# A two-layer decoder on one core: each layer's last residual as 7 products of sums, with the weights' sums made by DMA steps due by a rate for each stage

## The chip, the cores and the metric

The kernel runs on one core of one Trainium2 chip. The metric is the device time of one execution in microseconds (us), as the median of several runs. Five engines work side by side on the core: TensorE (PE: matrix products; PEld is its load of the stationary operand), VectorE (DVE), ScalarE (ACT), GpSimd (POOL) and SyncE (SP), which here only issues DMA transfers.

## The reference, cut to what matters

```python
for layer in range(2):
    h = rmsnorm(x, norm_mix[layer])                 # x: 512 tokens x 1024
    z = h @ w_in[layer]                             # then a convolution, two attentions, gates
    x = x + (g_conv * y_conv + g_attn * y_nsa + g_mla * y_mla) @ w_out[layer]
    x = x + memory_cross_attention(rmsnorm(x, norm_xattn[layer]), ...)
    gate, up = jnp.split(rmsnorm(x, norm_ffn[layer]) @ w_gate_up[layer], 2, axis=-1)
    x = x + (jax.nn.silu(gate) * up) @ w_down[layer]    # 512 x 2816 times 2816 x 1024
return rmsnorm(x, norm_final)
```

All data is float32. The line that the change rewrites is the product with `w_down`, once per layer; FFN below is the 2816.

## The kernel before, in words

Every float32 product is made as three matmuls of halves: each operand is split into a high part (a cast on ACT, `hilo`, L92) and a low part (the difference, on DVE, L93), and high times high, high times low and low times high are accumulated in one bank of PSUM (L85 to L87, or L1143 to L1145 in `residual`). Weights come through three steps. `load` (L101) brings up to 1 MB into `raw`, of which there are two buffers, by a DMA that SP issues. `unit` splits 128x1024 of it into `wh` and `wl`, three buffers each. Then PE uses them.

A layer goes through these stages: the mix (`mix`: projection, convolution, both attentions, merges), the residual with `w_out`, the cross attention and its residual, the feed forward (gate and up), and the last residual with `w_down`. Instructions on an engine run in program order, which a scheduler has fixed by priorities.

Gate and up are already computed with 7 products in place of 8 (a 2x2 scheme on sums of quarters of both operands). The sums of quarters of `w_gate_up` are made in DRAM by `summed`: 128 DMA steps per layer, each a copy or an accumulating copy of 320 KB, in groups of 8 in which the fifth and sixth add to what the first two left, the seventh adds the fifth's result and the eighth the seventh's. POOL issues them (L356). `tick` is called after each third matmul and yields one step at each fifth call in layer 0 and at each sixth for layer 1, whose steps begin in layer 0's last residual. Each step also waits on the matmul it was tied to. POOL has other work in its queue as well: fills of `Pc` (L879) and `PTh` for the attentions, the power in each norm (L200, tile `rs`) and the stores of `x` to DRAM (`xd`, L1298).

In the last residual, `residual` walks over 22 k-tiles of 128. Each k-tile's unit of 128x1024 weights feeds 4 token tiles and 2 column halves, so 8 accumulators x 3 = 24 matmuls of 128x512, 528 per layer. `act` holds the activations, already split, in buffers that `keep_act` fills during the feed forward; at the end 8 additions (L1157) put the banks on `xs`, and `after` stores them or makes the final norm.

Of the kernel before, what the change touches and what calls it, by code (L numbers as in the profile page):

```python
# [9 lines left out]
F32 = mybir.dt.float32  # L10
# [8 lines left out]
T = 512  # L19
# [32 lines left out]
def kernel(ctx, tc, x, mem, positions, rel_bias, norm_mix, norm_xattn, norm_mem, norm_ffn, norm_final,  # L52
# [276 lines left out]
    def summed(l):  # L329

        W = w_gate_up[l]
        n, rows = FFN - 256, 64
        sums = [dr.tile([512, n], F32, name=f"sums{l}_{i}") for i in range(4)]

        def steps():
            for r, c in pairs(range(0, 512, rows), (0, n // 2)):
                s = [t[r:r + rows, c:c + n // 2] for t in sums]
                w = [[W[q + r:q + r + rows, o + 256 + c:o + 256 + c + n // 2] for q in (0, 512)] for o in (0, FFN)]  # L340
                for dst, src in ((s[0], w[1][0]), (s[2], w[0][0]), (s[1], w[0][0]), (s[3], w[0][1])):
                    yield dst, src, None
                for dst, src in ((s[0], w[1][1]), (s[2], w[1][0]), (s[1], s[0]), (s[3], s[1])):
                    yield dst, src, OP.add

        return sums, steps()
# [3 lines left out]
    paced = {"count": 0, "every": 1, "steps": iter(())}  # L350

    def tick(product):
        paced["count"] += 1
        if paced["count"] % paced["every"] == 0:
            for dst, src, op in islice(paced["steps"], 1):
                d = nc.gpsimd.dma_start(dst, src, accum_op=op) if op else nc.gpsimd.dma_start(dst, src)  # L356
# [4 lines left out]
    def mix(l, x_src, g_mix, x_now, more_x):  # L361
# [10 lines left out]

        tm_raw = [tm_load(0)]
# [719 lines left out]

        for _ in start(1):
            pump(3)
# [17 lines left out]

        run(merge_steps(1, w_branch_nsa[l], split4([o_nsa[0][:, k, :] for k in range(4)])))
# [54 lines left out]

    xin = x[0]  # L1170
# [3 lines left out]
    sums, paced["steps"] = summed(0)  # L1174
    paced["every"] = 5
    for l in range(L):
# [126 lines left out]
        assert not list(paced["steps"])  # L1303
        g_next = load_gain(norm_final if last else norm_mix[l + 1])
        act = []
        homes = ["op"] * 10 + ["ca"] * 2 + ["PT"] * 2 + ["gm", "h", "h", "u"] + ["o8"] * 2 + ["BT"] * 2
        size = {"o8": 4, "BT": 2}
        shared = {}

        def act_slots(m):  # L1310
            home = homes[m]
            if home == "PT":
                return new("PTh", dt=F32R, name="ah"), new("PTl", dt=F32R, name="al")
            if home == "h":

                k = 2 * (m - homes.index("h"))
                return hTh[:, k:k + 2, 256:512], hTl[:, k:k + 2, 256:512]
            if home == "u":
                return [new("u", (128, T + TAPS - 1), F32R, name="au")[:, 0:T] for _ in range(2)]
            if home in ("o8", "BT"):  # L1320
                i = shared.setdefault(home, [None, 0])
                r = []
                for _ in range(2):
                    if i[0] is None:
                        i[0], i[1] = new(home, (128, size[home], 512), F32R, name="a4"), 0
                    r.append(i[0][:, i[1], :])
                    i[1] += 1
                    if i[1] == size[home]:
                        i[0] = None
                return r  # L1330
            return new(home, dt=F32R, name="ah"), new(home, dt=F32R, name="al")

        def keep_act(m, a):
            ah, al = act_slots(m)
            hilo(ah, al, a.rearrange("p (a b) -> p a b", a=2) if len(ah.shape) == 3 else a)
            act.append((ah, al))
# [101 lines left out]
        if not last:  # L1438
            sums, paced["steps"] = summed(1)
            paced["every"] = 6  # L1440
# [64 lines left out]
```

## Time and profile before

| | before |
|---|---|
| median of 3 runs | 1943.12 us (1942.74 to 1944.12) |
| the profiled execution | 1943.2 us, of which the span that the profile covers is 1941.5 us |
| PE busy | 1913.9 us, 99% of the span |
| DVE, ACT, POOL busy | 1371.0, 979.2, 227.6 us |
| DMA queue of SP (weights) and queue of POOL (steps, stores) | 34.8% and 21.0% of 16 engines' span |
| first to last matmul start of layer 0's last residual | 855.09 to 975.65 us |

The profiled execution lies 0.1 us above the median, so its times can be used without correction. A busy time counts each instruction's own duration; PE's matmuls overlap, and what one costs is the distance between two starts.

### The profile page before, as it was taken

The numbers are of one execution on the slowest core, as the hardware profiler recorded it, in microseconds if no ns is written. First come the engines' busy times: TensorE is split into PE (matmuls) and PEld (weight loads), VectorE is DVE, ScalarE is ACT, GpSimd is POOL, SyncE is SP. The second block draws the span as 40 slices with busy tenths as digits, with TensorE's granted clock in tenths as the row PEclk, the third lists the DMA queues.
The fourth block names the chain that finished last, engine by engine and source line by source line (L and its number), as shares of the span: only waits on it lengthen the run. The fifth ranks groups of instructions, "written<-read, shape, count | busy, mean of one in ns | idle before, by whom it ended". The sixth has DMA issues, their size and how long they took to land.

```text
span 1941.5 us, 29100 instructions
## 1 busy us (share of the span) xinstructions
PE 1913.9 (99%) x11136; PEld 1674.5 (86%) x11136; DVE 1371.0 (71%) x2525; ACT 979.2 (50%) x1858; POOL 227.6 (12%) x380
## 2 busy tenths in 40 slices
PE   9999999999999999999999999999999999999998
PEld 8877888888887999998888878888888889999886
DVE  6989899764466877762279989986655677777523
ACT  5366557663355545541244755675634465545312
POOL 1211112112121000001211111111112010000000
PEclk9999999999999999999999999999999999999999
DMA  6676655567783455566666565445676525555531
GB/s 186 152 188 182 154 134 137 132 169 211 221 229 113 154 175 192 177 226 176 175 168 162 161 189 127 122 102 141 170 204 181 177 99 173 179 182 174 183 108 65
DMA packets 218871, 317.95 MB, mean 164 GB/s; under 512 B 14528, under 2 KB 172483, under 8 KB 218732
## 3 DMA queue, kind: packets, MB, share of 16 engines
q1 hardware_dynamic: 194028, 220.83, 34.8%
q0 software_dynamic: 21760, 88.10, 21.0%
q10 hardware_dynamic: 2944, 7.17, 1.1%
q8 instruction: 87, 1.43, 0.3%
q14 instruction: 52, 0.43, 0.1%
HBM read 307.64 MB, written 92.30 MB: 206 GB/s over the span
## 4 chain that ended last, share of the span: by engine, by line
PE 80%; DVE 8%; issue 5%; DMA 4%; ACT 3%; POOL 1%; SPq 0%; DVEq 0%; POOLq 0%; ACTq 0%
PE ps_mm L85 12%; PE ps_mm L87 12%; PE ps_mm L86 12%; PE ps_mm L1143 2%; PE ps_mm L1144 2%; PE ps_mm L1145 2%; PE ps_t L85 2%; PE ps_t L86 2%; PE ps_t L87 2%; PE ps_s L85 2%; PE ps_s L86 2%; PE ps_s L87 2%; DMA raw<-in_w_in_dram 2%; PE ps_t L960 2%; PE ps_t L1144 2%
## 5 line engine op out<-in xcount | busy, mean ns | idle before, releaser
L93 DVE TENSOR_TENSOR wl<-raw,wh 128x1024 fp32r<-128x1024 f32 (+5 forms) x382 | 451.2, 1185 | 377.2 <-ACT wh L92 375.7
L92 ACT CAST wh<-raw 128x1024 fp32r<-128x1024 f32 (+5 forms) x382 | 388.0, 1020 | 587.5 <-PE ps_pv L1145 198.7
L85 PE MATMUL ps_mm<-hTh,wh 128*128 128x512 f32 (+1 forms) x1152 | 415.4, 361 | 1.1 <-DVE kc L93 1.1
L87 PE MATMUL ps_mm<-hTh,wl 128*128 128x512 f32 (+1 forms) x1152 | 411.4, 358 | 0.8 <-DVE wl L93 0.8
L86 PE MATMUL ps_mm<-hTl,wh 128*128 128x512 f32 (+1 forms) x1152 | 412.0, 358 | 0.0
L87 PEld LDWEIGHTS ps_mm<-hTh,wl 128*128 128x128 f32 x1152 | 218.2, 190 | 33.4 <-DVE wl L93 1.9
L85 PEld LDWEIGHTS ps_mm<-hTh,wh 128*128 128x128 f32 x1152 | 218.5, 190 | 30.4 <-DVE kc L93 1.5
L86 PEld LDWEIGHTS ps_mm<-hTl,wh 128*128 128x128 f32 x1152 | 218.5, 190 | 26.5 <-issue 0.7
L356 POOL DMA_DIRECT2D sums<-in_w_gate_up_dram x192 | 119.6, 627 | 842.1 <-PE ps_mm L87 429.6
L463 DVE SCALAR_TENSOR_TENSOR ca<-u,vT,ca 128x512 f32<-128x512 f32 x240 | 177.1, 745 | 2.9
L923 ACT ACTIVATE P<-P,ss 128x512 f32<-128x512 f32 (+3 forms) x128 | 71.4, 558 | 55.9 <-DVE ss L920 55.0
L92 ACT CAST PTh<-ps_t 128x512 fp32r<-128x512 f32 (+4 forms) x136 | 70.4, 517 | 55.8 <-PE ps_t L960 45.0
L85 PE MATMUL ps_s<-rh,wh 128*128 128x256 f32 x320 | 90.6, 283 | 0.0
L86 PE MATMUL ps_s<-rl,wh 128*128 128x256 f32 x320 | 90.6, 283 | 0.0
L87 PE MATMUL ps_s<-rh,wl 128*128 128x256 f32 x320 | 90.6, 283 | 0.0
L356 POOL DMA_DIRECT2D sums<-sums x64 | 50.0, 782 | 275.4 <-PE ps_mm L87 130.1
L93 DVE TENSOR_TENSOR PTl<-ps_t,PTh 128x512 fp32r<-128x512 f32 (+2 forms) x120 | 71.3, 596 | 8.4 <-ACT PTh L92 7.5
L931 ACT ACTIVATE P<-P,sr 128x512 f32<-128x512 f32 (+3 forms) x128 | 63.1, 553 | 18.2 <-DVE sr L929 18.1
L85 PE MATMUL ps_mm<-op,wh 128*128 128x512 f32 (+1 forms) x192 | 68.7, 358 | 0.0
L86 PE MATMUL ps_mm<-op,wh 128*128 128x512 f32 (+1 forms) x192 | 68.2, 355 | 0.0
L87 PE MATMUL ps_mm<-op,wl 128*128 128x512 f32 (+1 forms) x192 | 68.1, 355 | 0.0
L200 POOL TENSOR_TENSOR rs<-rs,mhalf 128x1 f32<-128x1 f32 x32 | 23.1, 721 | 383.5 <-DVE rs L197 383.3
(553 smaller groups left out, 4574.1 us busy)
## 6 DMA issues: line engine op xcount, KB each, us to landing
sums<-in_w_gate_up_dram POOLq DMA_DIRECT2D x192, 320.0 KB, 4.4
raw<-sums SPq DMA_DIRECT2D x80, 512.0 KB
raw<-in_w_in_dram SPq DMA_DIRECT2D x32, 1024.0 KB
raw<-in_w_gate_up_dram SPq DMA_DIRECT2D x24, 1024.0 KB
raw<-in_w_down_dram SPq DMA_DIRECT2D x22, 1024.0 KB
sums<-sums POOLq DMA_DIRECT2D x64, 320.0 KB, 4.9
raw<-in_w_in_dram SPq DMA_DIRECT2D x26, 512.0 KB
raw<-in_w_gate_up_dram SPq DMA_DIRECT2D x20, 512.0 KB
```

Of the source, the lines that this page charges most:

```text
L85: nc.tensor.matmul(o, lh, rh, start=start, stop=False)
L86: nc.tensor.matmul(o, lh, rl, start=False, stop=False)
L87: tick(nc.tensor.matmul(o, ll, rh, start=False, stop=stop))
L92: nc.scalar.copy(hi, src)
L93: nc.vector.tensor_tensor(lo, src, f(hi), op=OP.subtract)
L356: d = nc.gpsimd.dma_start(dst, src, accum_op=op) if op else nc.gpsimd.dma_start(dst, src)
L463: nc.vector.scalar_tensor_tensor(c, u[:, j:j + T], cw[:, m, j:j + 1], c, op0=OP.mult, op1=OP.add)
L923: nc.scalar.activation(p[:, c], p[:, c], AF.Exp, bias=s[:, k:k + 1], scale=-1.0, accum_out=s[:, 4 + k:5 + k])
L931: nc.scalar.activation(P[k], P[k], AF.Copy, scale=r[:, k:k + 1])
L960: nc.tensor.transpose(tp[:, w:w + 128], P[k][:, j * 128:(j + 1) * 128], ident)
L1143: nc.tensor.matmul(o, xh, wh[:, r], start=k == 0, stop=False)
L1144: nc.tensor.matmul(o, xh, wl[:, r], start=False, stop=False)
```

## The change

The last residual becomes `down_residual`. The output is cut into token halves (256 tokens) and column halves (512), and the 2816 long sum into 11 pairs of k-tiles. Seven parts run in turn, each with its own pair of operands: sums of quarters of the activations on one side, quarters or sums of quarters of `w_down` on the other. A part has 11 pairs x 2 token tiles x 3 = 66 matmuls of 128x512, so a layer has 462. Each part loads its weights anew, in loads of 1 MB, 1 MB and 0.75 MB, and splits them in 5.5 units. Its results go to `xs` by additions after each part (`done`), some through a held tile `U`.

The sums of `w_down`'s quarters are 88 further DMA steps per layer (256 KB each), behind the 128 of gate and up. `tick` now adds a rate per call and issues a step when 1.0 is reached: 0.25 at the start of the mix, 0.35 in the attentions, 0.25 from the last merge to the cross attention, 0.05 in the feed forward, 0.06 in layer 0's last residual, where layer 1's steps begin.

`keep_act` multiplies into unsplit quarters, splits only two of the four sums that it keeps, and adds the sums by four 128x512 DVE additions per 4 m (256 hidden columns each pair of m) at low priority. The other five sums of activations are split in `down_residual`, a part ahead (`fourth`, `split`).

```diff
+        W, V = w_gate_up[l], w_down[l]
         n, rows = FFN - 256, 64
-        sums = [dr.tile([512, n], F32, name=f"sums{l}_{i}") for i in range(4)]
+        up = [dr.tile([512, n], F32, name=f"up{l}_{i}") for i in range(4)]
+        down = [dr.tile([128, FFN // 256, 512], F32, name=f"down{l}_{i}") for i in range(4 if l in seven else 0)]
+        def added(s, w):
+            for dst, src in ((s[0], w[1][0]), (s[2], w[0][0]), (s[1], w[0][0]), (s[3], w[0][1])):
+                yield dst, src, None
+            for dst, src in ((s[0], w[1][1]), (s[2], w[1][0]), (s[1], s[0]), (s[3], s[1])):
+                yield dst, src, OP.add
...
+            for j in range(FFN // 256 if down else 0):
+                yield from added([t[:, j, :] for t in down],
+                                 [[V[(2 * j + e) * 128:(2 * j + e + 1) * 128, o:o + 512] for e in range(2)]
+                                  for o in (0, 512)])
...
-        paced["count"] += 1
-        if paced["count"] % paced["every"] == 0:
+        paced["due"] += paced["rate"]
+        if paced["due"] >= 1.0:
+            paced["due"] -= 1.0
...
+        paced["rate"] = 0.25
...
+        paced["rate"] = 0.35
...
+        paced["rate"] = 0.25
...
+    def down_residual(W, sums, kept, xs, more_x, after):
+        N = len(kept)
+        low = slice(0, 512), slice(512, 1024)
+        quarters = W.rearrange("(j e p) c -> e p j c", e=2, p=128)
+        b11, b12, b21, b22 = ([k[e][i] for k in kept] for e in range(2) for i in range(2))
+        e11, e21 = ([(k[e][2], k[e][3]) for k in kept] for e in range(2))
+        def split(v):
+            h, lo = (new("op", (128, 2, 256), F32R, name=n)[:, 0:v.shape[1], :] for n in ("th", "tl"))
+            hilo(h, lo, v)
+            return h, lo
+        def fourth(n):
+            v = new("P", (128, 2, 256), name="t2")[:, 0:b11[n].shape[1], :]
+            nc.vector.scalar_tensor_tensor(v, b11[n], -1.0, b22[n], op0=OP.mult, op1=OP.subtract)
+            return split(v)
...
+        parts = [(quarters[0][:, :, low[0]], lambda n: None), (quarters[1][:, :, low[0]], fourth), (sums[1], lambda n: split(b12[n])),
+                 (sums[2], lambda n: split(b21[n])), (quarters[1][:, :, low[1]], lambda n: split(b11[n])),
+                 (sums[0], lambda n: split(b22[n])), (sums[3], lambda n: None)]
+        tags = (("t", "t"), ("s", "s"), ("mm", "mm"), ("mm", "pv"), ("t", "t"), ("s", "s"), ("mm", "mm"))
+        U = [None] * 2
...
+        def done(i, t, p):
+            x, y = xs[t], xs[2 + t]
+            if i == 0:
+                U[t] = new("op", name="U")
+                nc.scalar.copy(U[t], p)
+                add(x[0], x[0], p)
+            elif i == 1:
+                add(x[0], x[0], p)
+            elif i == 2:
+                add(U[t], U[t], p)
+                later(y[0], U[t])
+            elif i == 3:
+                add(U[t], U[t], p)
+                later(x[1], U[t], OP.subtract)
+                later(y[1], U[t], OP.subtract)
+            elif i == 4:
+                add(x[1], x[1], p, OP.subtract)
+                after(t)
+            elif i == 5:
+                add(y[0], y[0], p)
+                add(y[1], y[1], p, OP.subtract)
+            else:
+                add(y[0], y[0], p)
+                after(2 + t)
...
+            def run(n, u, t):
+                for k in range(u[0].shape[1]):
+                    j = 2 * n + k
+                    xh, xl = (v[:, k, t * 128:(t + 1) * 128] for v in side[n])
+                    nc.tensor.matmul(accs[t], xh, u[0][:, k, :], start=j == 0, stop=False)
+                    nc.tensor.matmul(accs[t], xh, u[1][:, k, :], start=False, stop=False)
+                    tick(nc.tensor.matmul(accs[t], xl, u[0][:, k, :], start=False, stop=j == nj - 1))
+            held = []
+            for n in range(N):
+                j = 2 * n
+                if n % 2 == 0:
+                    m = min(4, nj - j)
+                    raw = load(lambda raw: [(raw.rearrange("p (k c) -> p k c", k=4)[:, 0:m], w[:, j:j + m, :])])
+                m = min(2, nj - j)
+                c = n % 2 * 1024
+                held.append((n, unit(raw[:, c:c + m * 512].rearrange("p (k c) -> p k c", k=m), (m, 512))))
+                then.append(ahead(n))
+                if n + 3 < N:
+                    for t in range(2):
+                        run(*held[0], t)
+                    held = []
+                elif i < 6 or n == N - 1:
+                    for t in range(2):
+                        for h in held:
+                            run(*h, t)
+                    held = []
+            if i == 0:
+                more_x()
+            for t in range(2):
+                done(i, t, accs[t])
+            if i == 0:
+                side = e21
+            else:
+                side = then
...
-        homes = ["op"] * 10 + ["ca"] * 2 + ["PT"] * 2 + ["gm", "h", "h", "u"] + ["o8"] * 2 + ["BT"] * 2
...
+        plain = iter(["op"] * 12 + ["u"] * 2 + ["o8"] * 4 + ["BT"] * 4)
+        halved = iter(["op"] * 8 + ["ca"] * 4 + ["PTh", "PTl"] * 2 + ["gm"] * 2 + ["h"] * 4)
...
+        def keep_act(m, a, b, sign=1.0):
+            d = act_slot(m)
+            for i in range(2):
+                q = slice(i * 256, (i + 1) * 256)
+                nc.vector.scalar_tensor_tensor(d[i], a[:, q], sign, b[:, q], op0=OP.mult, op1=OP.mult)
+            hilo(d[2], d[3], d[0])
+            if m % 4 == 3 or m == FFN // 128 - 1:
+                (b11, b12), (b21, b22) = (h[0:2] for h in kept[-1])
+                tc.cur_priority += 100000
+                nc.vector.tensor_tensor(b11, b11, b12, op=OP.subtract)
+                nc.vector.tensor_tensor(b21, b22, b21, op=OP.subtract)
+                nc.vector.tensor_tensor(b21, b21, b11, op=OP.add)
+                nc.vector.tensor_tensor(b12, b22, b12, op=OP.subtract)
...
-            paced["every"] = 6
...
+            sums, next_down, paced["steps"] = summed(1)
+            paced["issued"], paced["rate"] = 0, 0.06
...
-        residual(lambda k: act[k], FFN // 128, w_down[l], xs, after, 3 if last else 2, {8: lambda: load_x(xd, xs)})
+        xs = []
+        down_residual(w_down[l], down_sums, kept, xs, lambda: load_x(xd, xs), after)
```

Where it stands in the queues. On PE, in layer 0's last residual before: a unit `wh`/`wl` of weights (the number is the buffer's) against `ah`/`al`, the split activations of one k-tile, into the banks `ps_*`; the first two matmuls of a unit wait for ACT and DVE.

```order
L1143 MATMUL ps_t_9056<-wh_9395,ah_8062 128x512 [waits Activation_49]
L1144 MATMUL ps_t_9056<-wl_9396,ah_8062 128x512 [waits DVE_49]
L1145 MATMUL ps_t_9056<-wh_9395,al_8063 128x512
L1143 MATMUL ps_t_9057<-wh_9395,ah_8062 128x512
...
L1143 MATMUL ps_pv_9063<-wh_9395,ah_8062 128x512
...
L1143 MATMUL ps_t_9056<-wh_9424,ah_8081 128x512 [waits Activation_49]
```

And after, in the same stage (first part, from its fourth unit to its fifth):

```order
L1261 MATMUL ps_t_9198<-wh_9253,a_8179 128x512
L1262 MATMUL ps_t_9198<-wl_9254,a_8179 128x512
...
L1263 MATMUL ps_t_9199<-wh_9253,a_8180 128x512
...
L1261 MATMUL ps_t_9198<-wh_9271,a_8672 128x512 [waits Activation_49]
L1262 MATMUL ps_t_9198<-wl_9272,a_8672 128x512 [waits DVE_49]
L1263 MATMUL ps_t_9198<-wh_9271,a_8673 128x512
```

The two waits come with every unit in both, but the unit that before served 24 matmuls now serves 12, so PE asks for the next one after half as many.

On ACT, the casts of weight units (`wh` from `raw`) in the same stage before; each waits for its load (DMA), and for a free buffer (DVE, PE):

```order
L92 CAST wh_9334<-raw_9332 128x1024 [waits DMAHW7_49,DVE_49,PE_49]
L92 CAST wh_9364<-raw_9332 128x1024 [waits DVE_49,PE_49]
L92 CAST wh_9395<-raw_9393 128x1024 [waits DMAHW0_49,DVE_49,PE_49]
L92 CAST wh_9424<-raw_9393 128x1024 [waits DVE_49,PE_49]
L92 CAST wh_9456<-raw_9454 128x1024 [waits DMAHW1_49,DVE_49,PE_49]
```

And after, from the end of part 0 into part 1; `U` is the copy of a bank, `th` the high half of a sum of activations (`t2`) that the next part needs:

```order
L92 CAST wh_9346<-raw_9321 128x1024 [waits DVE_49,PE_49]
L1230 COPY U_9313<-ps_t_9198 128x512 [waits PE_49]
L1230 COPY U_9316<-ps_t_9199 128x512 [waits PE_49]
L92 CAST th_9329<-t2_9327 128x512
L92 CAST wh_9370<-raw_9368 128x1024 [waits DMAHW6_49,DVE_49]
L92 CAST th_9352<-t2_9350 128x512
L92 CAST wh_9392<-raw_9368 128x1024 [waits DVE_49,PE_49]
L92 CAST th_9376<-t2_9374 128x512
L92 CAST wh_9416<-raw_9414 128x1024 [waits DMAHW7_49,DVE_49,PE_49]
L92 CAST th_9398<-t2_9396 128x512
L92 CAST th_9422<-t2_9420 128x512
L92 CAST wh_9439<-raw_9414 128x512 [waits DVE_49,PE_49]
```

Between two casts of weights there now stands, as a rule, one of 128x512 for the next part.

On POOL, at the end of layer 0's cross attention before: the last steps, then the four norms' powers `rs` between the stores `xd`:

```order
L356 DMA sums0_1_148<-sums0_0_147 64x1280 [waits DMASW4_49,DMASW2_49,PE_49]
L356 DMA sums0_3_150<-sums0_1_148 64x1280 [waits DMASW6_49,DMASW7_49,DMASW3_49,PE_49]
L1298 DMA xd_134<-x_5034 128x512 [waits DVE_49]
L1298 DMA xd_134<-x_5036 128x512 [waits DVE_49]
L1298 DMA xd_134<-x_5038 128x512 [waits DVE_49]
L200 TENSOR_TENSOR rs_6188<-rs_6188,mhalf_72 128x1 [waits DVE_49,Pool_49]
L1298 DMA xd_134<-x_5040 128x512 [waits DVE_49]
L200 TENSOR_TENSOR rs_6229<-rs_6229,mhalf_72 128x1 [waits DVE_49,Pool_49]
L1298 DMA xd_134<-x_5042 128x512 [waits DVE_49]
L1298 DMA xd_134<-x_5044 128x512 [waits DMASW5_49,DVE_49]
```

And after, at the same place; `down` are the new sums in DRAM:

```order
L372 DMA down0_1_152<-down0_0_151 128x512 [waits DMASW5_49,DMASW1_49]
L372 DMA down0_0_151<-in_w_down_dram 128x512 [waits DMASW7_49,PE_49]
L372 DMA down0_3_154<-down0_1_152 128x512 [waits DMASW6_49,DMASW3_49]
L372 DMA down0_2_153<-in_w_down_dram 128x512 [waits PE_49]
L1420 DMA xd_134<-x_5093 128x512 [waits DVE_49]
L1420 DMA xd_134<-x_5095 128x512 [waits DVE_49]
L372 DMA down0_1_152<-in_w_down_dram 128x512 [waits DMASW4_49,PE_49]
L200 TENSOR_TENSOR rs_6266<-rs_6266,mhalf_72 128x1 [waits DVE_49,Pool_49]
L1420 DMA xd_134<-x_5097 128x512
L1420 DMA xd_134<-x_5099 128x512 [waits DVE_49]
L200 TENSOR_TENSOR rs_6308<-rs_6308,mhalf_72 128x1 [waits DVE_49,Pool_49]
L1420 DMA xd_134<-x_5101 128x512 [waits DMASW7_49,DVE_49]
```

The powers and stores, which had no step among them, now stand among steps that wait for a matmul (PE) and for earlier transfers (DMASW).

## Rows read from the trace of the kernel before

**Rows 1.** the page's head and busy time by engine
```profile
span 1941.5 us, 29100 instructions
...
PE 1913.9 (99%) x11136; PEld 1674.5 (86%) x11136; DVE 1371.0 (71%) x2525; ACT 979.2 (50%) x1858; POOL 227.6 (12%) x380
```

**Rows 2.** busy time by stretch of the span
```profile
core 0: us, PE busy (x) PEld busy (x) DVE busy (x) ACT busy (x) POOL busy (x), PEclk, DMA share, GB/s
200.00:300.00 100.00, 100.00 (x538) 84.86 (x537) 94.35 (x207) 59.62 (x123) 16.76 (x28) 1.00 0.60 146
490.00:522.00 32.00, 32.00 (x146) 26.22 (x145) 11.50 (x16) 8.52 (x15) 6.00 (x9) 1.00 0.79 243
...
606.00:855.00 249.00, 246.54 (x1975) 242.40 (x1974) 186.81 (x239) 128.43 (x203) 7.54 (x12) 0.99 0.53 176
855.00:970.00 115.00, 114.35 (x506) 94.34 (x505) 32.58 (x32) 26.13 (x30) 19.15 (x34) 1.00 0.67 182
1818.00:1932.00 114.00, 114.00 (x503) 93.99 (x502) 31.93 (x35) 25.10 (x33) 1.31 (x3) 1.00 0.26 95
```

**Rows 3.** PE's timeline, layer 0, middle of the last residual
```profile
899.80 0.39 PE L1144 MATMUL ps_t<-wl,ah 128*128 128x512 f32 x1
...
911.82 0.39 PE L1143 MATMUL ps_s<-wh,ah 128*128 128x512 f32 x1
```

**Rows 4.** PE's timeline, ends of the last residuals
```profile
855.09 0.39 PE L1143 MATMUL ps_t<-wh,ah 128*128 128x512 f32 x1
856.13 0.50 PE L1144 MATMUL ps_t<-wl,ah 128*128 128x512 f32 x1 [0.65 <-DVE wl L93]
...
975.65 0.39 PE L1145 MATMUL ps_pv<-wh,a 128*128 128x512 f32 x1
```

**Rows 5.** groups by line and shape, 855 to 970 us
```profile
L93 DVE TENSOR_TENSOR wl<-raw,wh 128x1024 fp32r<-128x1024 f32 x22 | 27.0, 1232 | 79.2 <-ACT wh L92 79.2
L92 ACT CAST wh<-raw 128x1024 fp32r<-128x1024 f32 x21 | 22.1, 1054 | 79.8 <-PE ps_pv L1145 79.4 <-DMA raw<-in_w_down_dram 0.4
```

**Rows 6.** costliest groups of the whole span, from the page
```profile
L463 DVE SCALAR_TENSOR_TENSOR ca<-u,vT,ca 128x512 f32<-128x512 f32 x240 | 177.1, 745 | 2.9
```

**Rows 7.** loads of raw around 705 us, issues
```profile
L101 SPq DMA_DIRECT2D raw<-in_w_gate_up_dram x2: 372/372/373, 699.2 to 704.9; - x2
```

**Rows 8.** ACT's timeline, the cast behind that load
```profile
709.99 1.05 ACT L92 CAST wh<-raw 128x1024 fp32r<-128x1024 f32 x1 [3.17 <-DMA raw<-in_w_gate_up_dram]
```

**Rows 9.** the chain that ended last, DMA entries
```profile
845.98 7.69 DMA raw<-in_w_down_dram
...
1803.82 7.39 DMA raw<-in_w_down_dram
```

**Rows 10.** DMA queue of the steps, from the page
```profile
q0 software_dynamic: 21760, 88.10, 21.0%
```

**Rows 11.** DMA issues at 855 to 970 us
```profile
sums<-in_w_gate_up_dram POOLq DMA_DIRECT2D x21, 320.0 KB, 4.2
```

**Rows 12.** DMA issues at 200 to 300 us
```profile
sums<-in_w_gate_up_dram POOLq DMA_DIRECT2D x16, 320.0 KB, 4.3
```

**Rows 13.** POOL's timeline, attention, then the cross attention's end
```profile
238.39 0.21 POOL L879 MEMSET Pc<- 128x128 f32 x1
...
617.45 1.68 POOL L1298 DMA_DIRECT2D xd<-x  x3 [35.15 <-DVE x L1157]
619.14 0.58 POOL L200 TENSOR_TENSOR rs<-rs,mhalf 128x1 f32<-128x1 f32 x1
```

**Rows 14.** waits, whole span: total, times, longest
```profile
POOL sums L356 <- DMA sums<-sums: 50.0, 11, 7.0
```

**Rows 15.** DVE's timeline, user of that Pc
```profile
241.36 0.36 DVE L882 TENSOR_TENSOR Pc<-ps_s,BT 128x46 f32<-128x46 f32 x2
```

**Rows 16.** PE's timeline, end of the cross attention's residual
```profile
620.56 1.01 PE L221 MATMUL ps_t<-ident,hn 128*128 128x128 f32 x4 [2.27 <-DVE hn L213]
...
622.50 0.77 PE L1145 MATMUL ps_mm<-wh,ox 128*128 128x512 f32 x1
```

More of the change, by code (lines that the diff above doesn't have):

```diff
@@ L346, in summed @@
-        return sums, steps()
+                yield from added([t[r:r + rows, c:c + n // 2] for t in up],
+                                 [[W[q + r:q + r + rows, o + 256 + c:o + 256 + c + n // 2] for q in (0, 512)]
+                                  for o in (0, FFN)])
+            for j in range(FFN // 256 if down else 0):
+                yield from added([t[:, j, :] for t in down],
+                                 [[V[(2 * j + e) * 128:(2 * j + e + 1) * 128, o:o + 512] for e in range(2)]
+                                  for o in (0, 512)])
@@ L1168, in load_x, with add, later @@
         return xs
+    def down_residual(W, sums, kept, xs, more_x, after):
[17 more added lines that the diff above has]
+        U = [None] * 2
+        def add(o, a, b, op=OP.add):
+            nc.vector.tensor_tensor(o, a, b, op=op)
+        def later(o, a, op=OP.add):
+            tc.cur_priority += 100000
+            add(o, o, a, op)
+            tc.cur_priority -= 100000
+        def done(i, t, p):
[22 more added lines that the diff above has]
+                after(2 + t)
+        nj = FFN // 256
+        side = e11
+        for i, (w, ahead) in enumerate(parts):
+            accs = [bank(tag) for tag in tags[i]]
+            then = []
+            def run(n, u, t):
[32 more added lines that the diff above has]
+                side = then
@@ L1173 @@
     xs = load_x(xin, [], (0,))
-    sums, paced["steps"] = summed(0)
-    paced["every"] = 5
+    sums, down_sums, paced["steps"] = summed(0)
     for l in range(L):
@@ L1302 @@
         last = l == L - 1
-        assert not list(paced["steps"])
+        assert paced["issued"] >= 128
+        paced["rate"] = 0.05
         g_next = load_gain(norm_final if last else norm_mix[l + 1])
-        act = []
-        homes = ["op"] * 10 + ["ca"] * 2 + ["PT"] * 2 + ["gm", "h", "h", "u"] + ["o8"] * 2 + ["BT"] * 2
[L1307 to L1336, printed above, removed]
+        plain = iter(["op"] * 12 + ["u"] * 2 + ["o8"] * 4 + ["BT"] * 4)
+        halved = iter(["op"] * 8 + ["ca"] * 4 + ["PTh", "PTl"] * 2 + ["gm"] * 2 + ["h"] * 4)
+        quarter = iter([h[:, k:k + 2, 256:512] for h in (hTh, hTl) for k in (0, 2)])
+        shared = {"o8": [], "BT": []}
+        def home(tags, dt):
+            tag = next(tags)
+            if tag == "h":
+                return next(quarter)
+            if tag in shared:
+                if not shared[tag]:
+                    n = 4 if tag == "o8" else 2
+                    t = new(tag, (128, n, 2, 256), dt, name="a4")
+                    shared[tag] += [t[:, i] for i in range(n)]
+                return shared[tag].pop(0)
+            if tag == "u":
+                return new("u", (128, T + TAPS - 1), dt, name="au")[:, 0:T].rearrange("p (j c) -> p j c", j=2)
+            return new(tag, (128, 2, 256), dt, name="a")
@@ L1448, in after @@
                     nc.sync.dma_start(out[0, t * 128:(t + 1) * 128, c * 512:(c + 1) * 512], h)
[L1449 removed]
+        xs = []
+        down_residual(w_down[l], down_sums, kept, xs, lambda: load_x(xd, xs), after)
+        if not last:
+            down_sums = next_down
         x_src = xd
```

36 lines of the change are left out of this document (20 added, 16 removed).

## The prediction

> **What bounds the kernel now.** I read the page's head first: PE is busy 1913.9 us of a span of 1941.5 [rows 1]. No other engine comes near, so only what changes PE's work, or makes PE wait, can move the time. The table of stretches says whether that holds in the stages that the change touches: PE is busy 114.35 of 115 us in layer 0's last residual, 114.00 of 114 in layer 1's, 246.54 of 249 in the feed forward, all of 100 in the densest part of the attention and all of 32 in the residual with `w_out`. DVE stands at 32.58 of 115 in the last residual but at 94.35 of 100 in that part of the attention, and the DMA engines at shares of 0.26 to 0.79 [rows 2]. So the stage that loses matmuls has large reserves on the other engines, while the stages that receive the new DMA steps have less.
>
> Since matmuls overlap, their price is the distance of starts: 53 of them lie between 899.80 and 911.82 [rows 3], 0.2268 us each. The last residual checks it: 528 x 0.2268 = 119.7 us, and with the one wait of 0.65 us for a unit's low half it should last 120.4; its first and last starts are 855.09 and 975.65, 120.6 apart [rows 4].
>
> **What is removed.** 462 matmuls of the same shape instead of 528 per layer: 66 x 0.2268 = 14.97 us, for two layers **-29.9 us**. Their operands have the same 128x512 shape, so I see no reason for another distance. This is the only gain.
>
> **The new last residual's side work.** A part lasts 66 x 0.2268 = 14.97 us. In it ACT casts 5.5 units at 1.054 us, 5.8 us, and DVE subtracts 5.5 at 1.232, 6.8 us [rows 5]. For the next part's activations there are 5.5 splits of 128x512, and about 3 additions of that size (22 a layer). The trace's nearest DVE instruction of this size took 745 ns [rows 6], so 8.5 x 0.745 = 6.3 us on DVE and, by the same bound, 4.1 on ACT. DVE: 13.1 of 15.0 us; ACT: 9.9. Neither becomes the bound; the feed forward already runs with DVE at 186.81 of 249 and hardly a wait on PE [rows 2]. But a unit now lasts 12 x 0.2268 = 2.72 us where it lasted 5.44, as PE's rows in the section on the change show, so side work that falls between two casts can make a unit late. From below nothing; from above some 0.6 us (the wait of [rows 4]) at each of 7 part changes, 4 us. The three buffers let splits run ahead, so I take a value near the lower end, **+1 us per layer**.
>
> **Its loads.** Each part reads 2.75 MB of 2^20 bytes, 2.88 million bytes in 14.97 us: 193 GB/s, against 182 and 95 moved in these stretches before, and 176 in the feed forward at a DMA share of 0.53 [rows 2]. The share follows as 0.53 x 193 / 176 = 0.58, plus 9 steps of layer 1. A step costs at most 0.21 x 1941.5 / 272 = 1.5 us of all 16 engines (queue of 256 steps and 16 stores) [rows 10], so they add 13.5 / 105 = 0.13: about 0.71. Bandwidth suffices. Latency is the question. `raw` has two buffers; one is refilled only when its second unit is split, so each buffer goes round in a load, its first cast and two subtractions (the second cast runs beside the first of them), the load plus 1.05 + 1.23 + 1.23 = 3.5 us [rows 5], and serves every second load. The time PE needs for two average loads is 14.97 x 2 / 3 = 9.98 us. In the feed forward a load issued at 704.9 [rows 7] let its cast begin at 709.99 [rows 8], 5.1 us: loop 8.6, below 9.98, nothing lost. I take 5.1, because that stage has the same demand and the same two buffers; the longer figure below is the rival.
>
> **The steps.** 88 more per layer, 88 x 1.5 = 132 us of the DMA engines, nearly all put into the mix, the residual with `w_out` and the cross attention. In layer 0 some 61 more than before fall into the first 490 us, 92 us or a share of 0.19 on top. At 0.79 PE still lost nothing in the stretch 490 to 522 [rows 2]. PE could lose something in the cross attention, where weights' loads and steps already meet. Bounds: nothing, and one load late by about 2.3 us (7.39 against 5.1) [rows 7 to 9] twice a layer, 5 us.
>
> POOL itself: 88 steps at about 0.6 us leave it far from busy, but its queue is in order, and a step that adds to another step's result waits until that has landed. The longest such wait was 7.0 us [rows 14]. What stands behind it is late by as much. A fill of `Pc` ended at 238.60 [rows 13], its reader on DVE began at 241.36 [rows 15]: 2.8 us of lead, so a blocked fill could cost DVE 4.2 us there, and there are 8 of them a layer. DVE's results reach PE some steps later, behind other ready products. From below 0, from above half of the 8, 17 us. I take loads and queue together as **+1 us per layer**, near the end that the table shows (no PE wait at all at 200 to 300).
>
> The Trainium skill speaks against this edit: in "SBUF — State Buffer", section "SBUF: two separate sides", a DMA that GpSimd issues needs GpSimd to write its descriptors, and certain VectorE instructions lock it out of the shared port until they end. By that rule each step in the attention would land late by up to one DVE instruction. The trace does not show it: steps landed in 4.3 us where DVE was 94% busy [rows 2, 12] and in 4.2 us where it was 28% busy [rows 11]; by the rule, with the 1.232 us of [rows 5] added to three landings in line, a group of 8 steps would block POOL about 3.7 us longer, and the sum would rise only where that reaches PE.
>
> **The norms behind the cross attention.** Before, the powers stood behind stores alone: stores at 617.45, the first power at 619.14 [rows 13], and PE waited 2.27 us for the normed rows, with a residual matmul of 0.77 us instead of 0.39 right after [rows 16]. Now steps stand among the four powers, as POOL's rows in the section on the change show, but some of the stores stand behind them. Counting the queue by hand at 0.6 us an issue puts the first power at 619.1 to 619.7. Cost 0, bounds -2 and +7 (one landing wait [rows 14]) per layer.
>
> **The feed forward and the ends.** Four additions of 0.745 us per 4 m, less what `keep_act` no longer splits, about +1.8 us of DVE per 40 us: 75% becomes 80%. PE hides it; without that cover it would be 1.8 x 5.5 = 10 us a layer. Two of the four token tiles are finished two parts early, so the last stores and norm have no more behind the last matmul than before: 0, within 0.7.
>
> **Sum.** 1943.2 - 29.9 + 2 x (1 + 1) = 1917.3, say **1917 us**. The profiled run is 0.1 above the median of the three.
>
> **The rivals.** *The loads are too slow.* The first load of the last residual took 7.69 us in layer 0 and 7.39 in layer 1 on the chain [rows 9], in company of the loads of `x`. If every load took 7.5, the loop would be 11.0 against 9.98, 1.0 us for two loads, with 21 loads a layer 10.7 us; both layers 21 us, 1938. It begins above a load of 6.5 us. For it: the share of 0.71 in layer 0. Against it: the feed forward at nearly the same rate.
>
> *Nothing waits.* Then 1943.2 - 29.9 = 1913.3. For it: no stage that the change touches shows PE idle by more than 1% in the table.
>
> *POOL's queue makes it slower than before.* Per layer 8 fills of `Pc` and 8 powers of the two residuals' norms stand among the steps; if each comes late by a landing wait less the lead, 7.0 - 2.8 = 4.2 us, and only half of that reaches PE, 32 x 2.1 = 67 us, so 1984. It decides the sign from 29.9 / 32 = 0.93 us each. For it: PE's 2.27 us behind such a power [rows 16], and DVE at 94%. Against it: the steps already ran there at a smaller rate, and PE waited for nothing from 200 to 300.
>
> **How the numbers follow.** What a measurement of this kernel tells from no change is about 0.2%, 3.9 us. The forecast (1914 to 1923) 0.58; slow loads, in part or wholly (1923 to 1939) 0.24; nothing waits (below 1914) 0.10; POOL's queue or other waits eat the gain, 0.08, of which 0.03 within 0.2% and 0.05 slower. Range 1911 to 1935: it leaves out the top of the slow loads, 0.04, and the last case's 0.08 above, and almost nothing below. Faster 0.92, same 0.03, slower 0.05.
>
> **What would show it.** In the profile after, the distance between the last residual's first and last matmul should be 104.8 to 107 us in each layer, with at most a few waits for `wl` or `wh`; 115 would be the loads, and the casts' idle time would name the DMA of `raw`. `Pc`'s readers should not name POOL, and PE's waits before the transposes at the cross attention's end should stay near 2 us. The prediction is wrong if the distance of matmul starts changes, or if the mix grows by more than 5 us in a layer.

## The result and the profile after

The changed kernel took 1952.56 us as the median of 13 runs (1945.2 to 1961.31), the kernel before 1943.11 beside it (1939.68 to 1944.15): a ratio of 1.0058 (95% interval 1.0048 to 1.0067). It is 9 us slower where 26 us less were forecast. The profiled execution, 1945.2 us, is the fastest of the 13, so the trace shows a good run of this kernel, and some 7 us of the median are in no trace. The runs spread over 16 us where those of before spread over 4.5.

The page's head, the DMA queues, and the shares of the chain that ended last:

```profile
span 1943.5 us, 29622 instructions
...
PE 1891.6 (97%) x11004; PEld 1649.1 (85%) x11004; DVE 1481.1 (76%) x2757; ACT 1037.1 (53%) x1962; POOL 347.0 (18%) x556
...
q0 software_dynamic: 41472, 134.25, 31.8%
...
PE 73%; DVE 10%; DMA 10%; ACT 4%; issue 2%; POOL 1%; SPq 0%; DVEq 0%; POOLq 0%; ACTq 0%
```

Against [rows 1], PE is busy 22.3 us less, yet the span is 2 us longer: PE now stands idle for 51.9 us instead of 27.6. The steps' queue went from 21.0% [rows 10] to 31.8%. In the chain the DMA share was 4% before.

Busy time by stretch of the kernel after (columns as in [rows 2]):

```profile
80.00:200.00 120.00, 113.25 (x590) 94.16 (x588) 105.06 (x215) 69.67 (x142) 27.02 (x44) 0.99 0.78 203
...
200.00:300.00 100.00, 99.56 (x533) 84.17 (x532) 94.14 (x204) 59.30 (x121) 26.12 (x44) 1.00 0.80 204
...
490.00:522.00 32.00, 32.00 (x150) 26.37 (x149) 14.00 (x20) 9.29 (x16) 8.39 (x13) 1.00 0.87 262
...
606.00:855.00 249.00, 243.66 (x1909) 236.35 (x1909) 190.77 (x285) 125.04 (x211) 22.52 (x33) 0.99 0.61 184
...
855.00:970.00 115.00, 112.61 (x548) 94.17 (x547) 91.96 (x126) 61.99 (x89) 8.92 (x18) 1.00 0.74 236
```

The attention from 200 us and the residual with `w_out` carry DMA shares of 0.80 and 0.87 and cost PE next to nothing, as forecast. The loss lies elsewhere. From 80 to 200 us PE is busy 113.25 of 120, and the prediction read no row of that stretch. Before, it was:

```profile
80.00:200.00 120.00, 115.05 (x607) 96.18 (x606) 108.88 (x225) 72.25 (x148) 19.82 (x33) 1.00 0.69 179
```

It already had waits, and a share of 0.69. What ends them is in the chain of the kernel after, entries of DMA:

```profile
116.18 6.91 DMA raw<-in_w_in_dram
...
128.38 7.47 DMA raw<-in_cmp_w_k_dram
...
152.76 7.75 DMA raw<-in_cmp_w_v_dram
...
549.34 8.76 DMA raw<-in_w_xq_dram
...
675.32 8.16 DMA raw<-in_w_gate_up_dram
...
859.90 7.66 DMA raw<-in_w_down_dram
...
1509.37 10.63 DMA raw<-in_w_xq_dram
```

These are loads of weights by SP that take 7 to 11 us, in four stages: the start of the mix, the cross attention, the feed forward and the last residual. Before, the chain had such loads too: those of the last residuals in [rows 9], and, among those that the prediction left out, one at the start of the mix:

```profile
95.75 8.65 DMA raw<-in_w_in_dram
```

To see where time is lost, I matched the n-th matmul of each source line in both traces and took the median difference of starts within 8 us of a mark (the mark is a time of the kernel before; positive is later). The runs below are those of the experiments:

```
mark (us)           75    200    606    850    982   1160   1500   1600   1800  last matmul
the change         0.0    4.5    9.9   13.9    2.5    5.8    7.7   14.3   13.6   -0.2
e1_stage_only      0.0    1.1    1.8    1.9    2.3    1.0    1.3    1.2    0.5  -13.4
e2_steps_only      0.0    9.1   14.0   15.3   14.7   24.1   29.0   37.0   36.4   36.1
e6_stage_alone     0.1    0.6    3.3    1.9  -13.4  -12.6  -11.0   -9.0   -9.6  -23.1
e7_rates_only      0.2   13.7   15.6   15.6   15.1   18.6   21.5   21.7   21.0   21.1
e3_narrow          0.2   13.9   17.0   17.1    4.5   12.2   14.0   14.8   14.1   -0.1
e4_plain           0.0    9.0   10.2    6.9   -5.4    3.3    4.8    7.2    6.5   -8.4
e9_later           0.1    0.9    5.5    1.9  -13.0   -9.9    0.7    8.5    7.8   -6.7
e10_narrow_up      0.0   -2.7    0.1   -1.3   -1.0   -3.5   -2.5   -2.2   -2.9   -3.0
e12_even           0.0   -1.2   -0.1    9.9   -5.7   -2.5    0.0    6.1   11.6   -4.1
```

The change loses 4.5 us by 200 us, 5.4 more to the end of the cross attention (by the same matching only 0.6 of them by 490 us, in the attention), 4 in the feed forward, gains 11.4 in the last residual, loses 11 again in layer 1 and gains 13.8 at its end.

### The profile page after: what moved, and what is told of

Read it like the earlier page. It is cut to its first block, busy times and chain, and to the rows that moved or that the text cites. A ratio compares the mean times of both kernels' runs of the same rounds, so it can differ in the third digit from the quotient of the medians.

```text
span 1943.5 us, 29622 instructions
## 1 busy us (share of the span) xinstructions
PE 1891.6 (97%) x11004; PEld 1649.1 (85%) x11004; DVE 1481.1 (76%) x2757; ACT 1037.1 (53%) x1962; POOL 347.0 (18%) x556
## 3 DMA queue, kind: packets, MB, share of 16 engines
q0 software_dynamic: 41472, 134.25, 31.8%
## 4 chain that ended last, share of the span: by engine, by line
PE 73%; DVE 10%; DMA 10%; ACT 4%; issue 2%; POOL 1%; SPq 0%; DVEq 0%; POOLq 0%; ACTq 0%
PE ps_mm L87 12%; PE ps_mm L85 12%; PE ps_mm L86 12%; DVE wl L93 3%; DMA raw<-in_w_in_dram 3%; PE ps_s L85 2%; PE ps_s L86 2%; PE ps_t L85 2%; PE ps_t L87 2%; PE ps_s L87 2%; PE ps_t L86 2%; ACT wh L92 2%; PE ps_t L977 2%; DVE ca L480 1%; DMA raw<-in_w_down_dram 1%
## 5 line engine op out<-in xcount | busy, mean ns | idle before, releaser
L92 ACT CAST wh<-raw 128x1024 fp32r<-128x1024 f32 (+3 forms) x422 | 423.1, 1008 | 498.4 <-PE ps_mm L86 116.2
L93 DVE TENSOR_TENSOR wl<-raw,wh 128x1024 fp32r<-128x1024 f32 (+3 forms) x422 | 491.3, 1170 | 252.7 <-ACT wh L92 251.1
L372 POOL DMA_DIRECT2D up<-in_w_gate_up_dram x192 | 123.3, 662 | 504.6 <-PE ps_mm L87 255.0
L372 POOL DMA_DIRECT2D down<-in_w_down_dram x132 | 90.8, 742 | 192.7 <-PE ps_mm L87 80.5
L372 POOL DMA_DIRECT2D up<-up x64 | 49.6, 775 | 232.6 <-DMA up<-up 80.6
L93 DVE TENSOR_TENSOR PTl<-ps_t,PTh 128x512 fp32r<-128x512 f32 (+2 forms) x120 | 71.6, 598 | 11.4 <-ACT PTh L92 10.6
L372 POOL DMA_DIRECT2D down<-down x44 | 36.0, 817 | 197.1 <-DMA down<-down 87.3
L85 PE MATMUL ps_mm<-op,wh 128*128 128x512 f32 (+1 forms) x192 | 68.7, 358 | 0.0
```

Source lines behind the costliest of these rows:

```text
L85: nc.tensor.matmul(o, lh, rh, start=start, stop=False)
L92: nc.scalar.copy(hi, src)
L93: nc.vector.tensor_tensor(lo, src, f(hi), op=OP.subtract)
```

## The experiments

The kernel before took 1941 to 1942 us (median) beside each group of runs.

**e1_stage_only** and **e6_stage_alone**: the new last residual without the steps it needs.

```diff
-            for j in range(FFN // 256 if down else 0):
+            for j in range(0):
...
-(sums[1], lambda n: split(b12[n]))
+(quarters[0][:, :, low[1]], lambda n: split(b12[n]))
```

The other three sums likewise; e1 has the rates 0.2 and then 1/6 throughout, e6 has 0.2 in the mix and 0 in layer 0's last residual.

> The change without the 88 further DMA steps per layer and with the pace of before (0.2, then 1/6); the four parts that read sums of w_down read plain quarters of it, so the work and the loads stay and only the sums are left out. Theory L (the steps' volume makes the weights' loads land late): the cost goes away, 1917 to 1922 us. Theory Q (POOL's in-order queue behind steps that wait for landings): the same 1917 to 1922. Theory S (the new last residual and the fuller feed forward cost what the matmuls save): about 1945 to 1952.

Measured: 1930.02 us (ratio 0.9935, 0.9911 to 0.9959), between the theories. The table shows why: layer 1's last residual gained 14 us, layer 0's nothing. My rate of 1/6 had put 25 steps of layer 1 there (29 in the kernel before, where the stage loads half as much). Its chain then runs from load to load, and PE waits for the halves:

```profile
868.99 7.33 DMA raw<-in_w_down_dram
...
880.48 5.62 DMA raw<-in_w_down_dram
...
890.25 5.71 DMA raw<-in_w_down_dram
...
899.57 7.90 DMA raw<-in_w_down_dram
...
908.77 5.08 DMA raw<-in_w_down_dram
...
917.80 9.26 DMA raw<-in_w_down_dram
```

```profile
905.20 0.50 PE L1261 MATMUL ps_mm<-wh,th 128*128 128x512 f32 x1 [1.41 <-ACT wh L92]
...
971.30 0.50 PE L1261 MATMUL ps_mm<-wh,th 128*128 128x512 f32 x1 [2.60 <-ACT wh L92]
```

The first is the chain, the second PE's timeline. From first to last matmul start the stage took 120.8 us, against 120.6 before [rows 4]: the rival of slow loads, in full, but with 25 steps in the stage. So I ran the stage without any step in it:

> The change without the 88 further steps, quarters of w_down in place of its sums (the sums are left out), the 128 steps at 0.2 in the mix and none in layer 0's last residual. P: 1913 to 1919, each last residual about 14 us shorter than before. If the new stage loses to its own side work: 1925 or more, with layer 0's stage again hardly shorter.

Measured: 1919.1 us (0.9887, 0.9871 to 0.9902), at the upper edge of what theory P expected. The stage takes 105.1 us in layer 0 and 107.0 in layer 1; in the changed kernel, with 9 steps in layer 0, 108.9 and 106.7. In e6 some 5 us are still lost in the two cross attentions (marks 606, 1500 to 1600), whose cause I did not separate.

**e2_steps_only** and **e7_rates_only**: the kernel before with the change's steps and rates, or with its rates alone for the 128 steps that it had.

```diff
-        if paced["count"] % paced["every"] == 0:
+        paced["due"] += paced["rate"]
+        if paced["due"] >= 1.0:
...
+        paced["rate"] = 0.25
...
+        paced["rate"] = 0.35
```

> The kernel before, with the 88 further steps per layer at the rates of the change, their result unused. L and Q: before plus 26 to 38 us, 1969 to 1981. S: 1943 to 1948.

Measured: 1981.34 us (1.0189, 1.0169 to 1.0209), just above the range of L and Q.

> The kernel before with the rates of the change (0.25, 0.35, 0.25, 0.05, 0.06) for its own 128 steps and no further step. P: the start of the mix is late by 3 to 10 us in each layer, 1949 to 1962 in all. N: 1941 to 1945.

Measured: 1964.5 us (1.0132, 1.0100 to 1.0163), 23.3 above the kernel before, without one added transfer, and more than P expected. 32 instead of 24 steps fall between 80 and 200 us; in this trace that stretch alone costs 13.5 us. Stretches and ACT's waits for loads in it, of e7:

```profile
80.00:200.00 120.00, 108.97 (x543) 89.22 (x542) 98.43 (x201) 66.12 (x134) 24.13 (x38) 0.96 0.71 179
...
120.00:140.00 20.00, 19.96 (x109) 17.11 (x108) 15.84 (x35) 14.29 (x32) 4.70 (x7) 1.00 0.97 245
140.00:200.00 60.00, 52.10 (x250) 42.16 (x250) 47.47 (x97) 34.83 (x74) 9.62 (x17) 0.91 0.62 156
...
148.00:152.00 4.00, 3.39 (x11) 2.71 (x12) 3.75 (x8) 2.01 (x5) 0.13 (x1) 0.65 0.10 23
...
160.00:164.00 4.00, 4.00 (x22) 3.37 (x21) 3.92 (x9) 2.27 (x4) 0.77 (x1) 1.00 0.99 238
```

```profile
ACT wh L92 <- DMA raw<-in_w_in_dram: 10.0, 4, 5.2
...
ACT w L92 <- DMA raw<-in_cmp_w_v_dram: 5.8, 2, 4.4
```

One load of `in_cmp_w_v`, and what it met, from the timelines of SP, POOL and ACT:

```profile
155.32 0.80 POOL L370 DMA_DIRECT2D up<-in_w_gate_up_dram  x1 [0.81 <-PE ps_mm L87]
157.27 0.37 SPq L101 DMA_DIRECT2D raw<-in_cmp_w_v_dram  x1
157.35 0.79 POOL L370 DMA_DIRECT2D up<-in_w_gate_up_dram  x1 [1.24 <-PE ps_mm L87]
160.94 0.77 POOL L370 DMA_DIRECT2D up<-up  x1 [2.80 <-PE ps_mm L87]
...
167.69 0.62 ACT L92 CAST w<-raw 128x512 fp32r<-128x512 f32 x1 [4.45 <-DMA raw<-in_cmp_w_v_dram]
```

The DMA engines are nearly full (0.97) from 120 to 140 us, nearly idle (0.10) from 148 to 152, and full again (0.99) from 160 to 164, where this load runs beside the steps issued around it; its cast begins 10.4 us after its issue. Over the 60 us from 140 on the engines are at 0.62: the work was not too much, it stood at the wrong time. Before, no wait for `in_cmp_w_v` was among the waits of this stretch, while those for `in_w_in` were about as long in sum and shorter at most:

```profile
ACT wh L92 <- DMA raw<-in_w_in_dram: 9.0, 6, 3.3
```

**e3_narrow, e4_plain, e10_narrow_up**: is it the steps' volume, or POOL's queue?

```diff
-                yield from added([t[:, j, :] for t in down],
+                yield from added([t[:, j, 0:64] for t in down],
```

> The change with each of the 88 steps cut to 64 of 512 columns (an eighth of the volume; same number, order, rates and waits), the parts reading plain quarters, so the sums are left out. L: 1918 to 1926, near the run without steps. Q: most of the cost stays, 1940 to 1952. S: 1945 to 1952.

Measured: 1941.91 us (0.9993, 0.9980 to 1.0006), outside what L expected and inside the range of Q, for I had not seen yet that the rates alone cost 23 us. With that known it fits: 1919.1 of e6 plus 23.3 of e7 is 1942.4. So 88 more steps of an eighth of the width, in the same order, cost nothing beyond the rates, and the change itself 11 us more. In the kernel before, the 88 steps at full width cost 16.8 beyond the rates (e2 against e7). Narrow steps also land sooner: POOL's waits for landings of `down` are 35.6 us in sum in e3's trace, 143.1 in the change's. (In e3 the last residual reads plain quarters, the sums are left out.) In e4 the 88 steps are replaced by copies:

```diff
-                yield from added([t[:, j, :] for t in down],
+                for _ in range(2):
+                    for i, (o, e) in enumerate(pairs((0, 512), range(2))):
+                        yield down[i][:, j, :], V[(2 * j + e) * 128:(2 * j + e + 1) * 128, o:o + 512], None
```

> The change with the 88 steps as independent plain copies of the same 256 KB, none of which waits for another's landing to add to it (the sums are replaced by copies of quarters). An accumulating step reads a third piece, so the volume falls by about a sixth. L: 1943 to 1952, most of the cost stays. Q: the cost goes, at most 1926. S: 1945 to 1952.

Measured: 1940.24 us (0.9990, 0.9974 to 1.0007), between the two. Copies of full width thus cost no more than narrow steps. The page counts the same bytes in POOL's queue as in the change (134.25 MB), while its packets' time falls from 31.8% to 28.2% and POOL's waits for landings of `down` from 143.1 to 10.2 us. So the width alone does not make the 88 steps dear; whether it is the additions' longer packets or the waits for their landings, no run tells apart. For the rates, where the loss is largest, the test is on the 128 steps (the sums of `w_gate_up` are left out):

```diff
-                yield from added([t[r:r + rows, c:c + n // 2] for t in up],
+                yield from added([t[r:r + rows, c:c + n // 16] for t in up],
```

> The kernel before with the rates of the change and no further step, as in the rates-only run (1964.5), but each of the 128 steps an eighth as wide, and the feed forward reading plain quarters of w_gate_up (its sums are left out). Volume of the steps as the cause (theory L): 1938 to 1947. POOL's queue, or the number of transfers (Q): 1955 to 1965.

Measured: 1941.66 us (0.9996, 0.9987 to 1.0006) against 1964.5 with full width. POOL issues as many transfers at the same places; the whole cost is gone. The stretch in e10:

```profile
80.00:200.00 120.00, 117.24 (x625) 98.35 (x624) 110.83 (x231) 73.59 (x150) 28.78 (x47) 1.00 0.47 129
```

POOL is busier than in e7 (28.78 against 24.13), the DMA share is 0.47, PE is busy 117.24. So the number of steps is not the cause. Narrow steps also land sooner (in 2.5 us against 4.8), and POOL's waits for landings fall from 66.5 to 28.1 us over the span, so e10 alone does not exclude those waits. The trace of e7 does for this stretch: POOL waits for landings there twice, 7.9 us in sum, none of PE's waits of 0.2 us and more names POOL, and those of ACT above name loads. The width of the steps, by way of late loads, is the cause of what the rates cost there.

**e5_repaced, e8_halves, e9_later, e11_later_halves, e12_even**: the change with other rates. e5 takes 0.15, 0.4, 0.2, 0.05 and 0 for the stages in order. e9 holds 0.2 until the compressed attention begins:

```diff
+            paced["rate"] = 0.2 if u < 4 else 0.45
             scores = start(u + 2 if u < 3 else u + 3)
```

e8 and e11 add to e5 and e9 that each load of the last residual is two transfers:

```diff
-                    raw = load(lambda raw: [(raw.rearrange("p (k c) -> p k c", k=4)[:, 0:m], w[:, j:j + m, :])])
+                    raw = load(lambda raw: [(raw.rearrange("p (k c) -> p k c", k=4)[:, q:min(q + 2, m)], w[:, j + q:j + min(q + 2, m), :]) for q in (0, 2)])
```

> The change with other rates alone: 0.15 instead of 0.25 up to the attentions, 0.4 instead of 0.35 in them, 0.2 instead of 0.25 behind them, 0.05 in the feed forward as before, none instead of 0.06 in layer 0's last residual. Theory P (steps cost where a stage's own weights' loads already fill the DMA engines: the start of the mix, the cross attention, the new last residual; in the attentions they are free): 1922 to 1934. Theory N (88 more steps cost the same wherever they stand): 1945 to 1955.

Measured: 1934.22 us (0.9967, 0.9954 to 0.9981): P, at its upper edge. Its rate of 0.4 begins where the change's 0.35 does, about 100 us into the layer, so 35 steps still fell between 80 and 200 us (36 in the change's trace).

> As the run with other rates, and each load of the new last residual as two transfers, one for each half of the buffer, so that a unit's cast can begin when its own half has landed. If loads that land late are what the stage still loses: 1 to 4 us below the run with other rates. If it is the splits: the same.

Measured: 1932.12 us (0.9959, 0.9944 to 0.9974). The intervals overlap: inconclusive for the whole. The stage itself is shorter: 104.8 and 104.7 us from first to last matmul start, where e5 has 105.8 and 106.0.

> The change with the dense rate only where the loads are few: 0.2 until the first compressed attention (about 200 us into a layer), 0.45 from there to the last merge, 0.2 behind it, 0.05 in the feed forward, none in layer 0's last residual. Theory P: the start of the mix is late by at most 1 to 2 us per layer, 1921 to 1929. If the steps cost by their number: 1934 or more, as in the repaced run before.

Measured: 1932.93 us (0.9953, 0.9937 to 0.9970), slower than P expected. The start of the mix is cured (0.9 us at the mark of 200), but at 0.45 the attentions are no longer free: in layer 1 the table shows 10.6 us between the marks of 1160 and 1500. The trace is that of the slowest of its 6 runs (1938.82); with the same rates e11's loses 3.5 us there. In both, PE waits for a fill that stands behind steps in POOL's queue. In e9, POOL's timeline, then PE's:

```profile
1378.03 0.78 POOL L372 DMA_DIRECT2D up<-up  x1 [6.02 <-PE ps_mm L87]
...
1379.95 0.52 POOL L957 MEMSET PTh<- 64x512 f32 x1
...
1380.53 0.79 PE L964 MATMUL ps_pv<-PTh,vc 128*128 128x512 f32 x1 [2.76 <-POOL PTh L957]
```

> As the run with the dense rate later, and the loads of the new last residual in two transfers each. If late loads are what that stage still loses (about 1 us per layer in the run without steps): 0 to 2 us below that run; otherwise the same.

Measured: 1930.7 us (0.9947, 0.9936 to 0.9959), the best of the runs with all of the computation; from e9 it cannot be told apart. Its stage takes 104.8 and 104.7 us, e9's 105.5 and 106.0.

> As the run with the dense rate later and halved loads, with 0.35 instead of 0.45 in the attentions and 0.09 instead of 0.05 in the feed forward, so that about 49 instead of 28 of a layer's 216 steps fall there. If the feed forward, whose loads have slack (51 to 53% DMA share), takes them for nothing and the attentions lose less: 1924 to 1930. If the feed forward's own loads then land late: 1931 to 1940.

From e11 it differs by two rates:

```diff
-            paced["rate"] = 0.2 if u < 4 else 0.45
+            paced["rate"] = 0.2 if u < 4 else 0.35
...
-        paced["rate"] = 0.05
+        paced["rate"] = 0.09
```

Measured: 1947.18 us (1.0022, 1.0011 to 1.0033). That is above both ranges. The attention and the feed forward of e12, and the latter in two pieces:

```profile
200.00:490.00 290.00, 289.53 (x1510) 243.34 (x1509) 224.01 (x509) 172.11 (x358) 70.37 (x115) 1.00 0.76 189
...
606.00:855.00 249.00, 239.60 (x1893) 233.47 (x1892) 187.70 (x272) 122.10 (x199) 42.55 (x64) 0.98 0.77 218
...
606.00:640.00 34.00, 26.90 (x134) 22.15 (x133) 18.77 (x29) 16.15 (x36) 11.56 (x20) 0.85 0.55 151
640.00:855.00 215.00, 212.71 (x1762) 211.31 (x1761) 168.93 (x243) 105.95 (x163) 30.99 (x45) 1.00 0.81 229
```

At the same share (0.76 and 0.77), PE loses 0.5 of 290 us in the one and 9.4 of 249 in the other. But 7.1 of the 9.4 lie before 640 us, at a share of 0.55, and most of them are one wait (2.27 us before, [rows 16]). POOL's timeline, then PE's:

```profile
620.10 0.80 POOL L372 DMA_DIRECT2D down<-down  x1 [7.86 <-DMA down<-down]
...
621.79 0.85 POOL L200 TENSOR_TENSOR rs<-rs,mhalf 128x1 f32<-128x1 f32 x1
...
623.49 1.11 PE L221 MATMUL ps_t<-ident,hn 128*128 128x128 f32 x4 [6.21 <-DVE hn L213]
```

The norm's power stood behind a step that waited for a landing: here POOL's queue costs more than the feed forward itself, where PE loses 2.3 of 215 us at a share of 0.81. In layer 1 the table shows 5.5 us between the marks of 1600 and 1800, so the feed forward does not take the steps for nothing either.

## Why the prediction was wrong

**What was right.** The removal was sized right: the stage without steps went from 120.6 to 105.1 and 107.0 us (forecast 104.8 to 107). PE's waits there are few; two of the longest of the kernel after, from PE's timeline:

```profile
870.02 0.50 PE L1262 MATMUL ps_t<-wl,a 128*128 128x512 f32 x1 [0.68 <-DVE wl L93]
...
886.72 0.50 PE L1262 MATMUL ps_s<-wl,a 128*128 128x512 f32 x1 [0.76 <-DVE wl L93]
```

So "+1 us per layer" for the side work stands in size without steps. But what it stood for seems to be loads rather than side work: with each load in two transfers and no step in the stage (e8, e11) it takes 104.7 to 104.8 us, and the 461 distances of 0.2268 alone make 104.6. The cross attention's end is a little later than forecast: PE waited 3.23 us instead of the 2.27 of [rows 16], and the first power, at 630.03, began 1 us later than the shift of the stage (9.9 us) explains. The prediction had put this term at 0, with bounds of -2 and +7.

```profile
631.45 1.09 PE L221 MATMUL ps_t<-ident,hn 128*128 128x128 f32 x4 [3.23 <-DVE hn L213]
```

```profile
630.03 0.59 POOL L200 TENSOR_TENSOR rs<-rs,mhalf 128x1 f32<-128x1 f32 x1
```

The first is from PE's timeline, the second from POOL's.

**What failed** is the step on the steps' price: "I take loads and queue together as +1 us per layer". In place of these 2 us in all, the runs show 23.3 for the rates (e7 against the kernel before) and 10.7 to 16.8 for the 88 steps (the change against e3, and e2 against e7). It went wrong in two ways. First, it priced only the 88 new steps. The change also gives the 128 old ones another place, because the rates 0.25 and 0.35 hold from the start of the mix; that alone is the +23.3 us of e7. The count was off too: 51 more steps than before fall into the first 490 us of the trace (151 against 100), not 61, and 31 instead of 19 into the 84 us behind 522, the cross attention. Secondly, it took its evidence from the stretches 200 to 300 and 490 to 522, where PE lost nothing at high shares, and added shares over 490 us. The stretch from 80 to 200 us was never read, although it had a share of 0.69 and PE waits before the change. The prediction's own sign, a mix that grows by more than 5 us in a layer, came: by the same matching, 5.1 us at a mark of 490 in the change's trace and 15.3 in that of e7.

By medians, -22.1 for the stage and its feed forward (e6) and +23.3 for the rates (e7) give +1.2, and e3, which has both, measured +0.5. The change has beyond e3 the full width of the 88 steps and the loading of their sums, +10.7 (from two groups of runs). That price is not fixed: by e6's -22.1 and e2's +39.9 the change should have come out at +17.8, and it measured +9.4.

**The rivals.** "The loads are too slow" was the right mechanism in a wrong place: I looked for it in the last residual, where 9 steps cost layer 0 about 3 us and 25 cost all of the gain (e1). The same kind of late load stood at the start of the mix and in the cross attention. "POOL's queue" is not what the start of the mix lost (e7 and e10), but it is not refuted: it acts at the two kinds of place that the prediction had named, a fill of the attention (e9) and the norms (e12), and in the change at the norm before the cross attention, where PE waited 0.98 us before:

```profile
535.14 0.81 POOL L372 DMA_DIRECT2D down<-down  x1 [5.90 <-DMA down<-down]
...
536.23 0.86 POOL L200 TENSOR_TENSOR rs<-rs,mhalf 128x1 f32<-128x1 f32 x1
...
537.93 0.66 PE L221 MATMUL ps_t<-ident,hn 128*128 128x128 f32 x4 [2.09 <-DVE hn L213]
```

These are single waits of 2 to 6 us, far from the 67 us that this rival had summed. As for the Trainium skill's rule on GpSimd's descriptors that was weighed ("SBUF — State Buffer"), e10 gives it no support here: POOL issues as many transfers beside a DVE that is busy 110.83 of 120 us, and nothing is lost. What the runs show is nearer to another page of the Trainium skill, "DMA: Bandwidth & Descriptors", section "Issuing engines are not separate DMA queues", which says that transfers of all issuing engines end up on the same 16 DMA engines and interleave; e7 against e10 agrees, 22.8 us apart by the width of POOL's transfers.

**Open.** Why the 88 steps cost what they do beyond the rates, by their additions' packets or by the waits for their landings, is not shown. Traces vary: up to 200 us e2, e7, e3 and e4 issue the same steps as the change, yet their traces are 9.1, 13.7, 13.9 and 9.0 us late there and the change's 4.5. I take this for most of the 7 us that the change's median lies above its trace, but no trace of a run near the median shows it. The last 2 us after the last matmul (8.1 us before, 10.3 after, with the same last matmul time) had been forecast as 0, within 0.7. About 1 us lies before the last normed rows, which DVE begins 4.2 us after the last matmul instead of 3.2; the cause of the rest is open.

## What to carry to other kernels

A background transfer is priced by the stage it falls in: at the start of the mix, where loads already ended waits, a denser pace (32 steps instead of 24 in 120 us) came with 13.5 us of delay in e7's trace, while 36 more steps in the attention (200 to 490 us) came with 0.6 in the change's. So when a pace is changed, count the steps of each stage before and after, old ones too, and read the stage where loads already end waits, not the one with spare room. Then look at the small work that stands behind a step in its issuer's queue. A stage that gains by fewer matmuls and more loads keeps its gain only if the background transfers stay out of it.

## What the runs showed of the hardware that was not expected

The granted TensorE clock fell behind the late loads: in e7 it is 0.91 in the 60 us from 140 to 200 (row above), where it was 1.00 before. Ahead of the longer of its two falls there, PE was busy 1.72 of 4 us, and its single waits there were at most 1.6 us:

```profile
172.00:176.00 4.00, 1.72 (x6) 0.82 (x5) 3.91 (x9) 2.53 (x7) 0.00 (x0) 1.00 0.79 240
176.00:180.00 4.00, 3.44 (x9) 2.32 (x10) 3.90 (x13) 2.42 (x7) 0.00 (x0) 0.57 0.63 214
```

Between the two levels, 1.2 and 2.4 GHz, a mean of 0.91 is 18% of the 60 us at the lower one, so an estimated 5 of the 13.5 us lost by then are matmuls at half speed after short waits of PE, not the waits themselves.
